# Two output products instead of three for four of eight scan tiles, with the scan's steps paced by VectorE's time

## The chip, the cores and the metric

One core of a Trainium2 chip runs the whole program. The metric is the device time of one execution in microseconds (us), as the median of several runs. Three runs of the kernel before gave 2316.76, 2317.06 and 2318.68 us, a median of 2317.06.

## The reference, cut to what matters

One decoder layer is computed for 304 tokens at once: 16 meta tokens, 256 prompt tokens, and 8 samples of 4 tokens. All of it is in fp32.

```python
x = x + 0.5 * swiglu(rmsnorm(x, norm_ffn1), ...)       # D 2048, D_FF 5632
z = rmsnorm(x, norm_mix) @ w_in                        # [u_pool | u_ssm | gate_a | gate_b]
a = pool_mix(u_pool)                                   # window means of 2, 4, 8, 16 tokens, minus u, times pool_w
s = s5_scan(u_ssm)                                     # below
s = gelu(s); s = s * sigmoid(s @ glu_w + glu_b)
m = sigmoid(gate_a) * (a @ w_branch_a) + sigmoid(gate_b) * (s @ w_branch_b)
x = x + m @ w_out
x = x + 0.5 * swiglu(rmsnorm(x, norm_ffn2), ...)
y = rmsnorm(x, final_norm)
# s5_scan: 64 groups of 16 channels, 64 complex states each
bu = einsum('blgc,gpc->blgp', u, b_bar)                # input product
h[t] = lam_bar * h[t-1] + bu[t]                        # complex, per state
y = einsum('blgp,gcp->blgc', h, c_mat).real + d * u    # output product
```

## The kernel before

**Weights.** Every weight matrix is read in blocks of 128x1024 in one fixed order (`weight_order`). SyncE's queue brings a block into one of `RAW` = 3 buffers (`raw`). ScalarE casts it to its high part (`whi`, line 161), and VectorE subtracts that from the block to get the rest (`wlo`, line 172). There are four buffers for each part. A *group* is the 24 matmuls that use one block: high part times high part, high times low, low times high (`mm3`, lines 252 to 254). Nearly all of TensorE's time goes into groups.

**Steps.** The program is recorded in an order written by hand; each engine runs its instructions in that order. After each group `step` records: the cast of the block three groups ahead (`high`), the work that waited for finished columns (`g.post`), the rest of that block (`low`), the next load, and then some *side work* from a generator. The rate `g.rate` says how many yields of the generator go into one step, one unit for one yield whatever it costs.

**The mixer.** `w_in`'s columns come first, in pairs of 128, in the order `COLS`: 0 to 3 feed the pooling branch and 4 to 7 the scan. Then come the four `pool_w` products, eight rounds of gate a with `w_branch_a` (six groups each), eight rounds of gate b (four groups each), the `glu_w` groups, and `w_branch_b`.

**The pooling.** `Pool.run` is side work on VectorE and ScalarE at 3.5 yields a step while the columns run. Its tiles are called `pt`, its results `Y`.

**The scan.** `Scan.run` is the side work after that, at `MIXRATE` = 1.53 yields a step, from the end of column 5 (the sixth of `COLS`). The states lie in 8 *row tiles* of two *halves*. A half is one tile `row` of three planes of 2x304: the input products `bu` of a tile fill planes 1 and 2 (`into`; ScalarE copies them out of PSUM). `rows` lists a half's eight steps, all on VectorE: a sum of planes 1 and 2 into plane 0 (608 elements a partition, line 965), all three planes times the rotation table `ee` (1824, line 966), a difference (1216, line 949, and a small line 951), two recurrences (`scan`, 608, line 955), a sum (576, line 971), all planes times the table again (1728, line 959: the *turned states*), and the final states out of them (36, line 962: `states`). The true parts of a state are differences of two of these planes. They are never formed for all tokens: the *output product* `outof` multiplies each of the three planes with its own 128x32 matrix and adds in PSUM (`yps`, line 914), 12 fp32 matmuls, which the profile counts as 24. It stands behind the third step of the next tile. `act` then puts gelu on it: seven small operations, to and fro between VectorE and ScalarE (`gy`, `gw`, `Y`).

Of the kernel before, what the change touches and what calls it, by code (L numbers as in the profile page):

```python
# [33 lines left out]
AHEAD = 2  # L34
RAW = 3
SETRATE = 1.25
MIXRATE = 1.53
WP = 1024
# [8 lines left out]
NCON = NT + NTV + 2  # L47
POOLRATE = 3.5
LATE = 8
STIR = 7  # L50
LAG = 0
MIXLAG = 2
COLS = (0, 1, 2, 4, 3, 5, 6, 7)
MAGIC = 12582912.0
# [128 lines left out]
def setup(ctx, tc, I):  # L183
    g = Ctx()
    nc = tc.nc
    g.tc, g.nc, g.I = tc, nc, I
    g.uid = 0
    g.side, g.rate, g.owed, g.post = None, 0, 0.0, []
# [12 lines left out]
    g.vec = g.const.tile([P, NVEC], F32, name="vec")  # L201
    return g
# [29 lines left out]

# [7 lines left out]
def also(g, more):  # L240
    g.side = more if g.side is None else chain(g.side, more)


def drain(g):
    while g.side is not None:
        if next(g.side, None) is None:
            g.side = None

# [590 lines left out]


class Scan:

# [8 lines left out]
    def input(self, ps, r):  # L851

        u = self.sp.tile([P, NT], F32, name=nm(self.g, "u"))
        self.g.nc.vector.tensor_tensor(u, ps, r, ALU.mult)
        self.u.append(u)
        if len(self.u) == 1:
            self.stored(0)
            self.stacked(0)
# [17 lines left out]
    def stored(self, i):  # L876

        g, nc = self.g, self.g.nc
        hi = self.sp.tile([P, NT], F32R, tag="uhi", name=nm(g, "uhi"), bufs=1)
        lo = self.sp.tile([P, NT], F32R, tag="ulo", name=nm(g, "ulo"), bufs=1)  # L880
        nc.scalar.copy(hi, self.u[i])
        nc.vector.tensor_tensor(lo, self.u[i], hi.bitcast(F32), ALU.subtract)
        for k, u in enumerate((hi, lo)):
            nc.gpsimd.dma_start(g.usc[i][k], u)
# [8 lines left out]
    def into(self, i, pair, ri, half, long=False):  # L893

        g = self.g
        if "row" not in pair[half]:
            pair[half]["row"] = self.sp.tile([P, 3, JB, NT], F32, tag="row", name=nm(g, "row"), bufs=4)
        row = pair[half]["row"][:, 1 + ri]
        for jj in range(JB):
            q = half * JB + jj  # L900
            ps = bank(g, "bu", aux=True, pool=g.pslong if long and jj else None)[:, :NT]
            g.nc.tensor.matmul(ps, self.bs[i][:, q, ri * P:(ri + 1) * P], self.up[:, q], start=True, stop=True)  # L902
            g.nc.scalar.copy(row[:, jj], ps)

    def outof(self, i, pair):
# [3 lines left out]
        c = self.cs[i].rearrange("p i (q c) -> p i q c", c=32)  # L909
        for k, h in enumerate((2, 1, 0)):  # L910
            for half, s in enumerate(pair):
                for jj in range(JB):
                    q = half * JB + jj
                    g.nc.tensor.matmul(self.yps[i][q * 32:q * 32 + 32], c[:, h, q], s["row"][:, h, jj, NMETA:],  # L914
                                       start=k == 0, stop=k == 2)

# [16 lines left out]
    def rows(self, sb, s):  # L933
# [23 lines left out]
        def back():  # L957
            x, e = (y.rearrange("p k j t -> p (k j) t")[:, :, NMETA:] for y in (row, ee))
            tt(x, x, e, ALU.mult)

        def states():
            tt(self.st[:, :, :, js].rearrange("p r k j -> p r j k"), both(one[:, :, S0 - 1::NS]),
               two[:, :, :, S0 - 1::NS], ALU.subtract)

        return [lambda: tt(fl(one), fl(two[:, 0]), fl(two[:, 1]), ALU.add),
                lambda: tt(row.rearrange("p k j t -> p (k j t)"), row.rearrange("p k j t -> p (k j t)"),
                           ee.rearrange("p k j t -> p (k j t)"), ALU.mult),
                turned,
                lambda: scan(2),
                lambda: scan(1),  # L970
                lambda: tt(one[:, :, NMETA:], two[:, 1, :, NMETA:], two[:, 0, :, NMETA:], ALU.add),
                back,
                states]

# [17 lines left out]
    def run(self):  # L992
# [4 lines left out]
        for i in range(KW):  # L997
            nxt = [{} for _ in range(half)]
            for h in range(half):
                sb = i * half + h  # L1000
                rows = self.rows(sb, pair[h])
                if sb >= 1 and sb + 1 < nb:
                    new = self.load(sb + 1)
                    (nxt[0] if h else pair[1])["ee"] = new["ee"]
                for n, row in enumerate(rows):
                    row()
                    if h == 0 and n == 2 and done is not None:
                        self.outof(i - 1, done)
                        acts = self.act(i - 1)
                    if h == 0 and n == 5 and i + 1 < KW:  # L1010
                        self.matrices(i + 1, ins=False)
                    k, late = divmod(h * len(rows) + n - 4, 3)
                    if i + 1 < KW and late == 0 and 0 <= k < 4:
                        self.into(i + 1, nxt, 1 - k % 2, k // 2)
                    if h == 0 and n == 1 and i + 2 < KW:
                        self.stored(i + 2)
                    if h and n == 6 and i + 2 < KW:
                        self.stacked(i + 2)
                        self.matrices(i + 2, outs=False)
                    while acts and h * len(rows) + n >= acts[0][0]:  # L1020
                        acts.pop(0)[1]()
                    yield 1
            done, pair = pair, nxt
        for _ in range(3):
            yield 1
        self.outof(KW - 1, done)
        yield 1
        for n, f in self.act(KW - 1):
            f()
            if n in (5, 7):  # L1030
                yield 1

# [5 lines left out]
class Pool:  # L1038


    def __init__(self, g, O):
# [9 lines left out]
        t2 = T()  # L1051
        self.f = [cut(t2, 0), cut(t2, 1)]
        self.LE = LE

# [3 lines left out]
    def run(self, p, pss, norm, out):  # L1058
# [6 lines left out]
        for u, end in zip(self.u, e):  # L1065
            nc.scalar.copy(end[:, :, HIST:], u[:, S0:].rearrange("p (b s) -> p b s", s=NS))
        yield 1
        for f in range(2):
# [4 lines left out]
    def means(self, w, u, e, out):  # L1073
# [4 lines left out]
        while k < w:  # L1078
# [3 lines left out]
            s, es, k, a = s2, e2, 2 * k, a ^ 1  # L1082
            yield 1
# [3 lines left out]
        yield 1  # L1087
        out.append(split(g, d, NL, "Y"))
        yield 1

# [7 lines left out]
def mixer(g, norm, O, ps0):  # L1098
# [8 lines left out]
    def gate(ps, c):  # L1107
        z = Z()[:, :NL]
        nc.vector.tensor_tensor(z, ps, norm.r[:, NMETA:], ALU.mult)
        nc.scalar.activation(z, z, AF.Sigmoid, bias=vcol(g, "b_gate", c))  # L1110
        return z

    with ExitStack() as cm:
        g.mix = cm.enter_context(g.tc.tile_pool(name="mix", bufs=1))
        with ExitStack() as cs:
# [3 lines left out]
            dparts, aparts = [], []  # L1119
            g.side, g.rate = None, POOLRATE  # L1120
            def spare(c):
                if c == KD // KC - 1:
                    g.owed -= MIXLAG

            for p in COLS:
                if p < KW // 2:
                    pool.fetch(p)
                before = {KW // 2 + 1: scan.begin, KW - 1: spare}.get(p)
                ps = proj(g, "w_in", p * 256, norm.x, NT, KD, before) if p else ps0
# [3 lines left out]
                else:  # L1133
                    g.post += [lambda q=q: scan.input(q, norm.r) for q in ps]
                if p == 1:
                    scan.first()
                if p == KW // 2 + 1:
                    drain(g)
                    g.side, g.rate = scan.run(), MIXRATE
                    g.owed = -LAG * MIXRATE  # L1140
            def mixed():
                g.owed -= MIXLAG
                for q in range(4):
# [4 lines left out]
                    for f in range(2):  # L1148
                        ps = bank(g, "pw")[:, :NL]
                        for k in range(2):  # L1150
# [3 lines left out]
                        g.post.append(lambda i=2 * q + f, ps=ps: aparts.append(  # L1154
                            split(g, ps, NL, "Y", vcol(g, "pool_scale", i))))
                    if q % 2:
                        step(g)

            mixed()
            for p in range(KD // 2):  # L1160
# [5 lines left out]
                def gated(p=p, z=z, pa=pa):  # L1166
                    for f in range(2):
                        nc.vector.tensor_tensor(z[f], pa[f], z[f], ALU.mult)
                        nc.sync.dma_start(msc[2 * p + f], z[f])

# [337 lines left out]
```

## Time and profile before

| what | value |
|---|---|
| median of three runs | 2317.06 us |
| the profiled execution's own time | 2318.77 us |
| its span | 2316.8 us |
| TensorE busy | 2306.3 us, 100% of the span |
| VectorE busy | 1576.1 us, 68% |
| ScalarE busy | 942.9 us, 41% |
| matmul records of the output products | 192, in eight bursts of 24 |

The profiled execution lies 1.71 us above the median of the three runs, and 1.97 us above its own span. The share of VectorE is an average: by the page's fortieths of the span it is busy for 40 to 80% in most of the program, and 90% or more of five of them in the middle. That is the mixer, from about 985 to 1290 us, and there the change works.

### The profile page before, as it was taken

What the parts mean: (1) busy time and instruction counts of PE and PEld (TensorE: products, weight loads), DVE (VectorE), ACT (ScalarE), POOL (GpSimd) and SP (SyncE); (2) the same over time, 40 slices, a digit from 0 to 9 for tenths busy, and PEclk for the clock granted to TensorE, in tenths of its full rate; (3) what the DMA queues carried; (4) which work ended last, traced back from release to release, by engine and by line L of the source; (5) the groups of instructions that cost most, each with busy time, mean ns of one, the idle gap of its engine ahead of it and who ended that gap; (6) DMA issues with size and microseconds to landing.
All of it is one profiled execution on the core that took longest, in us unless ns stands there. A gap on an engine that the chain in (4) does not pass through costs nothing.

```text
span 2316.8 us, 41582 instructions
## 1 busy us (share of the span) xinstructions
PE 2306.3 (100%) x17073; PEld 2293.3 (99%) x17073; DVE 1576.1 (68%) x2303; ACT 942.9 (41%) x1316; POOL 134.8 (6%) x255
## 2 busy tenths in 40 slices
PE   9999999999999999999999999999999999999998
PEld 9999999999999999999999999999999999999998
DVE  7788777877654557799999765545555555555556
ACT  5333333343333335454444544433333333333333
POOL 0000000002200002211110130000000000000001
PEclk9999999999999999999999999999999999999999
DMA  6445555556654446767785775444444444444543
GB/s 230 160 151 188 197 209 205 189 202 212 203 174 160 156 155 214 238 220 246 258 265 199 235 264 175 163 167 162 172 164 166 167 168 164 164 165 166 169 159 128
DMA packets 133454, 437.36 MB, mean 189 GB/s; under 512 B 22064, under 2 KB 33632, under 8 KB 133136
## 3 DMA queue, kind: packets, MB, share of 16 engines
q1 hardware_dynamic: 107088, 375.51, 47.6%
q0 software_dynamic: 25792, 58.87, 8.4%
q8 instruction: 134, 2.20, 0.4%
q14 instruction: 56, 0.46, 0.1%
q10 hardware_dynamic: 384, 0.32, 0.0%
HBM read 403.07 MB, written 31.55 MB: 188 GB/s over the span
## 4 chain that ended last, share of the span: by engine, by line
PE 98%; DVE 1%; issue 0%; ACT 0%; DMA 0%; SPq 0%; ACTq 0%; DVEq 0%
PE pj L253 24%; PE pj L252 24%; PE pj L254 24%; PE dn L254 8%; PE dn L252 8%; PE dn L253 8%; PE yps L914 1%; PE bu L902 0%; DMA pk<-in_first 0%; PE o L1245 0%; DVE row L955 0%; DVE wlo L172 0%; PE pw L253 0%; PE pw L252 0%; PE pw L254 0%
## 5 line engine op out<-in xcount | busy, mean ns | idle before, releaser
L172 DVE TENSOR_TENSOR wlo<-raw,whi 128x1024 fp32r<-128x1024 f32 (+1 forms) x697 | 849.6, 1220 | 576.5 <-ACT whi L161 575.6
L161 ACT CAST whi<-raw 128x1024 fp32r<-128x1024 f32 (+1 forms) x697 | 729.1, 1048 | 1202.6 <-PE pj L253 690.7
L252 PE MATMUL pj<-X,whi 128*128 128x304 f32 (+1 forms) x2428 | 728.3, 300 | 0.7 <-ACT whi L151 0.7
L253 PE MATMUL pj<-X,whi 128*128 128x304 f32 (+1 forms) x2428 | 728.2, 300 | 0.0
L254 PE MATMUL pj<-X,wlo 128*128 128x304 f32 (+1 forms) x2428 | 727.8, 300 | 0.0
L253 PE MATMUL pj<-Y,whi 128*128 128x288 f32 x1728 | 510.6, 296 | 0.0
L252 PE MATMUL pj<-Y,whi 128*128 128x288 f32 x1728 | 509.4, 295 | 0.0
L254 PE MATMUL pj<-Y,wlo 128*128 128x288 f32 x1728 | 508.8, 294 | 0.0
L252 PEld LDWEIGHTS pj<-X,whi 128*128 128x128 f32 x2428 | 457.2, 188 | 4.0 <-issue 2.1
L253 PEld LDWEIGHTS pj<-X,whi 128*128 128x128 f32 x2428 | 456.6, 188 | 0.1
L254 PEld LDWEIGHTS pj<-X,wlo 128*128 128x128 f32 x2428 | 456.3, 188 | 0.2
L252 PEld LDWEIGHTS pj<-Y,whi 128*128 128x128 f32 x1728 | 325.1, 188 | 0.9 <-issue 0.5
L253 PEld LDWEIGHTS pj<-Y,whi 128*128 128x128 f32 x1728 | 324.9, 188 | 0.0
L254 PEld LDWEIGHTS pj<-Y,wlo 128*128 128x128 f32 x1728 | 324.6, 188 | 0.0
L254 PE MATMUL dn<-H,wlo 128*128 128x304 f32 x704 | 213.0, 303 | 0.0
L252 PE MATMUL dn<-H,whi 128*128 128x304 f32 x704 | 212.8, 302 | 0.0
L253 PE MATMUL dn<-H,whi 128*128 128x304 f32 x704 | 212.2, 301 | 0.0
L254 PE MATMUL dn<-X,wlo 128*128 128x288 f32 x688 | 203.0, 295 | 0.0
L253 PE MATMUL dn<-X,whi 128*128 128x288 f32 x688 | 203.0, 295 | 0.0
L252 PE MATMUL dn<-X,whi 128*128 128x288 f32 x688 | 202.7, 295 | 0.0
L253 PEld LDWEIGHTS dn<-H,whi 128*128 128x128 f32 x704 | 132.4, 188 | 0.0
L252 PEld LDWEIGHTS dn<-H,whi 128*128 128x128 f32 x704 | 132.3, 188 | 0.0
(278 smaller groups left out, 1816.5 us busy)
## 6 DMA issues: line engine op xcount, KB each, us to landing
raw<-in_ffn_w_gate SPq DMA_DIRECT2D x175, 512.0 KB, 3.3
raw<-in_ffn_w_up SPq DMA_DIRECT2D x175, 512.0 KB, 3.3
raw<-in_ffn_w_down SPq DMA_DIRECT2D x168, 512.0 KB, 3.3
raw<-in_w_in SPq DMA_DIRECT2D x96, 512.0 KB, 4.3
raw<-in_w_out SPq DMA_DIRECT2D x32, 512.0 KB, 3.9
esc<-ee POOLq DMA_DIRECT2D x16, 912.0 KB, 5.7
ee<-esc POOLq DMA_DIRECT2D x16, 912.0 KB, 5.9
raw<-in_w_branch_a SPq DMA_DIRECT2D x16, 512.0 KB, 4.2
```

The source lines that it names most:

```text
L161: self.g.nc.scalar.copy(hi[:, :kn], self.raw[i][:, :kn])
L172: self.g.nc.vector.tensor_tensor(lo[:, :kn], raw[:, :kn], hi[:, :kn].bitcast(F32), ALU.subtract)
L252: mm(ps, wh, x[0], start=start, stop=False)
L253: mm(ps, wh, x[1], start=False, stop=False)
L254: mm(ps, wl, x[0], start=False, stop=stop)
L914: g.nc.tensor.matmul(self.yps[i][q * 32:q * 32 + 32], c[:, h, q], s["row"][:, h, jj, NMETA:], start=k == 0, stop=k == 2)
```

## The change

Five parts.

1. For row tiles 3, 4, 5 and 6 (`DIRECT`) the eighth step subtracts plane 0 from planes 1 and 2 over all 288 live tokens (1152 elements a partition, line 985). ScalarE then copies the final states with a sign (line 986) and `outof` needs two planes, 8 matmuls where it had 12.
2. Each yield returns its cost in us of VectorE, and a step's budget is the time of a group less the rest of a block: 3.186 - 1.135 us for 288 tokens, 3.355 - 1.135 for 304. VectorE's other work is taken off the budget where it is recorded, and TensorE's scan products are added to it.
3. The columns stand in the order 0, 4, 1, 5, 2, 3, 6, 7, so the scan begins after the fourth of them and no longer after the sixth. The pooling has a lane of its own (`front`) that goes first; nothing is drained at the scan's begin.
4. Four raw buffers for three.
5. The pooling's result tiles are taken at its begin.

```diff
-RAW = 3
+RAW = 4
-MIXRATE = 1.53
+LOWUS, SHORTUS, LONGUS = 1.135, 3.186, 3.355
+TIGHT = 0.0
+DIRECT = (3, 4, 5, 6,)
-COLS = (0, 1, 2, 4, 3, 5, 6, 7)
+COLS = (0, 4, 1, 5, 2, 3, 6, 7)
...
 def step(g):
...
     g.owed += g.rate
     while g.owed >= 1.0:
-        g.owed -= 1.0
-        got = next(g.side, None) if g.side is not None else None
-        if got is None:
-            g.side = None
+        cost = ahead(g)
+        if cost is None:
+            g.owed = min(g.owed, 1.0)
+            break
+        g.owed -= cost
+def ahead(g):
+    for lane in ("front", "side"):
+        gen = getattr(g, lane)
+        cost = next(gen, None) if gen is not None else None
+        if cost is not None:
+            return cost
+        setattr(g, lane, None)
...
     def outof(self, i, pair):
-        for k, h in enumerate((2, 1, 0)):
+        used = (2, 1) if i in DIRECT else (2, 1, 0)
+        g.owed += 0.54 * len(used)
+        for k, h in enumerate(used):
...
     def rows(self, sb, s):
+        def direct():
+            x = two[:, :, :, NMETA:]
+            tt(x, x, both(one[:, :, NMETA:]), ALU.subtract)
+            nc.scalar.activation(st, two[:, :, :, S0 - 1::NS], AF.Copy, scale=-1.0)
+        last = (1.33, direct) if sb * JB // 4 in DIRECT else (0.14, states)
...
+                (1.59, turned),
+                (1.335, lambda: scan(2)),
+                (1.335, lambda: scan(1)),
...
+                (1.88, back),
+                last]
...
 def mixer(g, norm, O, ps0):
-            g.side, g.rate = None, POOLRATE
+            g.side, g.rate = None, LONGUS - LOWUS
...
                 if p == KW // 2 + 1:
-                    drain(g)
-                    g.side, g.rate = scan.run(), MIXRATE
-                    g.owed = -LAG * MIXRATE
+                    g.side, g.owed = scan.run(), 0.0
+            g.rate = SHORTUS - LOWUS - TIGHT
```

How the order of instructions moves is shown at three places. On TensorE, before, the output product of row tile 3, between two groups (`row` and `cs` are its planes and matrix):

```order
L254 MATMUL pj_12719<-X_9555,wlo_12616 128x288
L914 MATMUL yps_12756<-row_11939,cs_11978 32x288 x2
L914 MATMUL yps_12756<-row_12098,cs_11978 32x288 x2
L914 MATMUL yps_12756<-row_11939,cs_11978 32x288 x2
L914 MATMUL yps_12756<-row_12098,cs_11978 32x288 x2
L914 MATMUL yps_12756<-row_11939,cs_11978 32x288 x2
L914 MATMUL yps_12756<-row_12098,cs_11978 32x288 x2
L252 MATMUL pj_12718<-X_9602,whi_12662 128x288
```

and now:

```order
L262 MATMUL pj_12514<-X_9752,wlo_12507 128x288
L931 MATMUL yps_12624<-row_11775,cs_11784 32x288 x2
L931 MATMUL yps_12624<-row_11934,cs_11784 32x288 x2
L931 MATMUL yps_12624<-row_11775,cs_11784 32x288 x2
L931 MATMUL yps_12624<-row_11934,cs_11784 32x288 x2
L260 MATMUL pj_12513<-X_9798,whi_12539 128x288
```

One plane of two halves is gone, four matmuls of twelve; so it is in tiles 4, 5 and 6.

On VectorE, before, at the end of a half of a middle tile (`z` are gate columns, `gw` a step of `act`):

```order
L172 TENSOR_TENSOR wlo_12873<-raw_12752,whi_12871 128x1024
L959 TENSOR_TENSOR row_12383<-row_12383,ee_12476 128x6x288
L927 SCALAR_TENSOR_TENSOR gw_12770<-gw_12770,gy_12769 128x288
L962 TENSOR_TENSOR states<-row_12383 128x2x2x9
L1109 TENSOR_TENSOR z_12915<-pj_12718,rs_y_10103 128x288
L1109 TENSOR_TENSOR z_12918<-pj_12719,rs_y_10103 128x288
L172 TENSOR_TENSOR wlo_12921<-raw_12801,whi_12913 128x1024
```

and now, at the end of tile 3's first half:

```order
L976 TENSOR_TENSOR row_11775<-row_11775,ee_11866 128x6x288
L944 SCALAR_TENSOR_TENSOR gw_12154<-gw_12154,gy_12153 128x288
L171 TENSOR_TENSOR wlo_12267<-raw_12136,whi_12265 128x1024
L985 TENSOR_TENSOR row_11775<-row_11775 128x4x288
L1195 TENSOR_TENSOR z_12225<-pj_12197,z_12225 128x288
L1195 TENSOR_TENSOR z_12228<-pj_12198,z_12228 128x288
L171 TENSOR_TENSOR wlo_12312<-raw_12186,whi_12306 128x1024
```

The difference of 1152 elements stands where the small one of 36 stood. Two gate products stand between it and the next rest in five of the eight halves; in the other three (tile 5's second, both of tile 6) the next rest follows at once. On ScalarE the copy of the states stands ahead of the cast for that rest.

On VectorE, now, at the scan's first half, between the columns of the pooling (`pt`, `Y`: pooling; `row`: scan):

```order
L1108 TENSOR_TENSOR pt_10012<-pt_10011 128x265
L1109 TENSOR_TENSOR pt_10015<-pt_10015 128x8x12
L1112 SCALAR_TENSOR_TENSOR pt_10010<-pt_10011,pt_10009 128x256
L1113 SCALAR_TENSOR_TENSOR pt_10010<-pt_10015,pt_10013 128x32
L1118 TENSOR_TENSOR Y_10027<-pt_10010,Y_10026 128x288
L976 TENSOR_TENSOR row_10396<-row_10396,ee_10209 128x6x288
L171 TENSOR_TENSOR wlo_10834<-raw_10718,whi_10832 128x1024
L981 TENSOR_TENSOR states<-row_10396 128x2x2x9
L989 TENSOR_TENSOR row_10403<-row_10403 128x608
L990 TENSOR_TENSOR row_10403<-row_10403,ee_10211 128x1824
```

Before, all of the pooling stood ahead of the scan's first instruction. From the scan's first instruction on VectorE to its last full step, the order now has 93 rests for 86 before, and 92 groups on TensorE for 85.

More of the change, by code (lines that the diff above doesn't have):

```diff
@@ L240, in also @@
 def also(g, more):
-    g.side = more if g.side is None else chain(g.side, more)
+    g.front = more if g.front is None else chain(g.front, more)
 def drain(g):
-    while g.side is not None:
-        if next(g.side, None) is None:
-            g.side = None
+    while ahead(g) is not None:
+        pass
 def mm3(g, ps, wh, wl, x, start, stop):
@@ L838, in ssm_setup @@
                     yield 1
+INTO = (4, 7, 10, 13)
+VIEWED = (5, 7, 9)
 class Scan:
@@ L854, in input @@
         self.g.nc.vector.tensor_tensor(u, ps, r, ALU.mult)
+        self.g.owed -= 0.38
         self.u.append(u)
@@ L882, in stored @@
         nc.vector.tensor_tensor(lo, self.u[i], hi.bitcast(F32), ALU.subtract)
+        g.owed -= 0.39
         for k, u in enumerate((hi, lo)):
@@ L903, in into @@
             g.nc.scalar.copy(row[:, jj], ps)
+            g.owed += 0.14
     def outof(self, i, pair):
@@ L914, in outof @@
                     g.nc.tensor.matmul(self.yps[i][q * 32:q * 32 + 32], c[:, h, q], s["row"][:, h, jj, NMETA:],
-                                       start=k == 0, stop=k == 2)
+                                       start=k == 0, stop=k == len(used) - 1)
     def act(self, i):
@@ L959, in back @@
             tt(x, x, e, ALU.mult)
+        st = self.st[:, :, :, js].rearrange("p r k j -> p r j k")
         def states():
[L962 to L973, printed above, removed]
+            tt(st, both(one[:, :, S0 - 1::NS]), two[:, :, :, S0 - 1::NS], ALU.subtract)
+        def direct():
[3 more added lines that the diff above has]
+        last = (1.33, direct) if sb * JB // 4 in DIRECT else (0.14, states)
+        return [(0.70, lambda: tt(fl(one), fl(two[:, 0]), fl(two[:, 1]), ALU.add)),
+                (1.97, lambda: tt(row.rearrange("p k j t -> p (k j t)"), row.rearrange("p k j t -> p (k j t)"),
+                                  ee.rearrange("p k j t -> p (k j t)"), ALU.mult)),
+                (1.59, turned),
+                (1.335, lambda: scan(2)),
+                (1.335, lambda: scan(1)),
+                (0.70, lambda: tt(one[:, :, NMETA:], two[:, 1, :, NMETA:], two[:, 0, :, NMETA:], ALU.add)),
+                (1.88, back),
+                last]
     def first(self):
@@ L1004, in run @@
                     (nxt[0] if h else pair[1])["ee"] = new["ee"]
-                for n, row in enumerate(rows):
+                for n, (cost, row) in enumerate(rows):
                     row()
-                    if h == 0 and n == 2 and done is not None:
+                    at = h * len(rows) + n
+                    if at == 2 and done is not None:
                         self.outof(i - 1, done)
                         acts = self.act(i - 1)
-                    if h == 0 and n == 5 and i + 1 < KW:
+                    if at == 5 and i + 1 < KW:
                         self.matrices(i + 1, ins=False)
-                    k, late = divmod(h * len(rows) + n - 4, 3)
-                    if i + 1 < KW and late == 0 and 0 <= k < 4:
+                    if i + 1 < KW and at in INTO:
+                        k = INTO.index(at)
                         self.into(i + 1, nxt, 1 - k % 2, k // 2)
-                    if h == 0 and n == 1 and i + 2 < KW:
+                    if at == 1 and i + 2 < KW:
                         self.stored(i + 2)
-                    if h and n == 6 and i + 2 < KW:
+                    if at == 14 and i + 2 < KW:
                         self.stacked(i + 2)
                         self.matrices(i + 2, outs=False)
-                    while acts and h * len(rows) + n >= acts[0][0]:
-                        acts.pop(0)[1]()
-                    yield 1
+                    while acts and at >= acts[0][0]:
+                        n, f = acts.pop(0)
+                        f()
+                        cost += 0.0 if n in VIEWED else 0.39
+                    yield cost
             done, pair = pair, nxt
-        for _ in range(3):
-            yield 1
+        for _ in range(2):
+            yield 2.0
         self.outof(KW - 1, done)
-        yield 1
+        yield 1.5
         for n, f in self.act(KW - 1):
             f()
-            if n in (5, 7):
-                yield 1
+            if n in VIEWED[:2]:
+                yield 1.5
     def store(self, O):
@@ L1052, in __init__ @@
         self.f = [cut(t2, 0), cut(t2, 1)]
+        self.parts = [(part(g, "Y", NL), part(g, "Y", NL)) for _ in range(KW)]
         self.LE = LE
@@ L1066, in run @@
             nc.scalar.copy(end[:, :, HIST:], u[:, S0:].rearrange("p (b s) -> p b s", s=NS))
-        yield 1
+        yield 0.77
         for f in range(2):
@@ L1086, in means @@
             ALU.mult, ALU.subtract)
-        yield 1
-        out.append(split(g, d, NL, "Y"))
-        yield 1
+        yield 0.45
+        hi, lo = self.parts[len(out)]
+        g.nc.scalar.copy(hi, d)
+        tt(lo, d, hi.bitcast(F32), ALU.subtract)
+        out.append((hi, lo))
+        yield 0.37
     def keep(self, p):
@@ L1109, in gate @@
         nc.vector.tensor_tensor(z, ps, norm.r[:, NMETA:], ALU.mult)
+        g.owed -= 0.37
         nc.scalar.activation(z, z, AF.Sigmoid, bias=vcol(g, "b_gate", c))
@@ L1127, in mixer @@
                     pool.fetch(p)
-                before = {KW // 2 + 1: scan.begin, KW - 1: spare}.get(p)
+                before = scan.begin if p == KW // 2 + 1 else None
                 ps = proj(g, "w_in", p * 256, norm.x, NT, KD, before) if p else ps0
@@ L1155, in mixed @@
                             split(g, ps, NL, "Y", vcol(g, "pool_scale", i))))
+                        g.owed -= 0.40
                     if q % 2:
```

14 lines of the change are left out of this document (4 added, 10 removed).

## The prediction

> **What bounds the kernel now.** I read the page's first lines, then TensorE's waits, then the scan's stretch.
>
> ```profile
> PE 2306.3 (100%) x17073; PEld 2293.3 (99%) x17073; DVE 1576.1 (68%) x2303; ACT 942.9 (41%) x1316; POOL 134.8 (6%) x255
> ...
> DVE  7788777877654557799999765545555555555556
> ...
> PE 98%; DVE 1%; issue 0%; ACT 0%; DMA 0%; SPq 0%; ACTq 0%; DVEq 0%
> ```
>
> TensorE is never idle; a change gains only by taking work from it. After the program's begin the list of TensorE's waits has one row inside the mixer:
>
> ```profile
> PE yps L914 <- DVE row L959: 0.5, 1, 0.5
> ```
>
> But VectorE, 68% over the span, is full in five fortieths. What counts there is its *lead*: how long before TensorE's first use a rest `wlo` is ready. From the timelines, the rests paired with their groups in order, three pairs (start us, us): at the scan's first half, at the lowest point, at the scan's last half.
>
> ```profile
> 979.74 1.22 DVE L172 TENSOR_TENSOR wlo<-raw,whi 128x1024 fp32r<-128x1024 f32 x1
> ...
> 988.14 0.30 PE L252 MATMUL pj<-X,whi 128*128 128x304 f32 x1
> ...
> 988.42 0.30 PE L254 MATMUL pj<-X,wlo 128*128 128x304 f32 x1
> ...
> 988.70 0.30 PE L253 MATMUL pj<-X,whi 128*128 128x304 f32 x1
> ...
> 1238.32 1.21 DVE L172 TENSOR_TENSOR wlo<-raw,whi 128x1024 fp32r<-128x1024 f32 x1
> ...
> 1239.10 0.29 PE L253 MATMUL pj<-X,whi 128*128 128x288 f32 x1
> ...
> 1239.63 0.36 PE L254 MATMUL pj<-X,wlo 128*128 128x288 f32 x1
> ...
> 1279.16 1.22 DVE L172 TENSOR_TENSOR wlo<-raw,whi 128x1024 fp32r<-128x1024 f32 x1
> ...
> 1282.48 0.29 PE L254 MATMUL pj<-X,wlo 128*128 128x288 f32 x1
> ```
>
> The lead is 7.46 us (988.42 less 980.96), then 0.10, then 2.10. The kernel before lives just inside VectorE's limit: the chain of waits leaves TensorE there and runs over VectorE and ScalarE to the product that waited.
>
> ```profile
> 1240.68 1.23 DVE wlo L172
> 1241.91 1.88 DVE row L959
> 1243.83 1.65 PE yps L914 x20
> ```
>
> VectorE's own stretch between the first and the last of those rests, from the table by windows and its waits there:
>
> ```profile
> 980.96:1280.38 299.42, 298.91 (x2315) 290.55 (x2313) 286.22 (x320) 144.84 (x236) 36.20 (x68) 1.00 0.74 237
> ...
> DVE wlo L172 <- ACT whi L161: 10.1, 12, 1.4
> ```
>
> Of 299.4 us VectorE (third pair) works 286.2 and stands 13.2; 10.1 of that in 12 waits for a cast. TensorE's 85 groups took 294.1 (988.42 to 1282.48). The difference, 5.4, is the lead that went.
>
> **Two output products.** This is the gain. TensorE's chain has a burst of 24 records, and what the next matmul takes after one:
>
> ```profile
> 1062.70 1.59 PE yps L914 x24
> 1064.29 0.33 PE pj L252
> ```
>
> A record takes 1.59 / 24 = 0.066 us. Four tiles lose 8 each, 32 x 0.066 = 2.1 us. The 0.33 behind a burst stays, as all eight bursts do. With the 0.5 that TensorE waited, 2.6 us can be had, and no more.
>
> **The difference on VectorE.** Durations overlap a little, so I take starts. Nearest are the sum of 576 elements, the rest and the states, and beside them the form of 1216:
>
> ```profile
> 1109.76 0.75 DVE L971 TENSOR_TENSOR row<-row 128x576 f32<-128x576 f32 x1
> 1110.43 0.82 DVE L1109 TENSOR_TENSOR z<-pj,rs_y 128x288 f32<-128x288 f32 x2
> ...
> 1114.67 1.22 DVE L172 TENSOR_TENSOR wlo<-raw,whi 128x1024 fp32r<-128x1024 f32 x1
> 1115.81 0.22 DVE L962 TENSOR_TENSOR states<-row 128x36 f32<-128x36 f32 x1
> 1115.94 0.79 DVE L965 TENSOR_TENSOR row<-row 128x608 f32<-128x608 f32 x1
> ...
> 1117.02 0.82 DVE L1168 TENSOR_TENSOR z<-pj,z 128x288 f32<-128x288 f32 x2
> 1117.75 1.22 DVE L172 TENSOR_TENSOR wlo<-raw,whi 128x1024 fp32r<-128x1024 f32 x1
> ...
> L949 DVE TENSOR_TENSOR row<-row 128x1216 f32<-128x1216 f32 x16 | 22.7, 1419 | 0.1
> ```
>
> A rest takes 1.14 from start to start, the states 0.13, a pair of `z` 0.73, and every instruction hands over some 0.08 before its end. 1152 elements lie between 576 (0.67 from start to start) and 1216 (1.42 less 0.08): 1.30, from 1.27 to 1.35. Eight of them cost 10.4, the eight states saved 1.1.
>
> A page of the Trainium skill speaks against all such counts: VectorE: DVE Perf Modes, "The DRAIN you can't avoid", says that the next instruction does not start until the pipe is empty. By it each instruction would take its full duration, 320 x 0.08 = 26 us more in this stretch, and TensorE would have waited over 20 us before the change. The trace has 0.5, and a rest of 1.22 is followed after 1.14; the measurement decides, and the sum stays.
>
> **The earlier scan.** The order now has 92 groups from the scan's first rest to its last where it had 85, since the scan starts two columns earlier. TensorE: 192 matmuls of 304 more, 24 of 288 fewer (0.140 and 0.133 from start to start: 988.14 to 988.70 and 1239.10 to 1239.63 are four each), 56 product records fewer (32 gone, 24 of the last tile behind the end), one turn behind a burst fewer, 0.2: 294.1 + 26.9 - 3.2 - 3.7 - 0.2 = 313.9 us. VectorE: seven rests more, 8.0; two `z` fewer, -0.7; the pooling of the columns 2 and 3, that stood ahead of the scan. Its 12 forms from 905 to 985 us, first and last:
>
> ```profile
> L278 DVE TENSOR_TENSOR Y<-pt,Y 128x288 fp32r<-128x288 f32 x8 | 3.7, 458 | 3.5 <-ACT Y L277 3.5
> ...
> L1081 DVE TENSOR_TENSOR pt<-pt 128x32 f32<-128x32 f32 x2 | 0.4, 186 | 0.0
> ```
>
> Those two columns' 44 instructions are 15.7 us of the 12 forms' 26.1, less 44 x 0.08: 12.2. So VectorE has 286.2 + 8.0 - 0.7 + 12.2 + 10.4 - 1.1 = 315.0 us of work beside 313.9 of TensorE's. That is what the new budget says by itself: costs equal to the starts above, 100% of the time, with nothing left for standing. Before, it was 286.2 of 294.1.
>
> **Standing.** Keep the 13.2. Then VectorE needs 328.2, and TensorE's time with a lead of 7.5 gives 321.4: TensorE waits 6.8 us for rests. Whether those waits go is seen from what ScalarE did ahead of them. Twice the cast itself waited for its raw block, elsewhere it mostly stood behind small steps of the scan:
>
> ```profile
> 1063.52 1.05 ACT L161 CAST whi<-raw 128x1024 fp32r<-128x1024 f32 x1 [5.01 <-DMA raw<-in_w_in]
> 1064.60 1.23 DVE L172 TENSOR_TENSOR wlo<-raw,whi 128x1024 fp32r<-128x1024 f32 x1 [1.00 <-ACT whi L161]
> ...
> 1078.28 0.45 ACT L928 ACTIVATE gw<-gw 128x288 f32<-128x288 f32 x1 [3.08 <-DVE gw L927]
> 1078.62 1.03 ACT L161 CAST whi<-raw 128x1024 fp32r<-128x1024 f32 x1
> 1079.69 1.23 DVE L172 TENSOR_TENSOR wlo<-raw,whi 128x1024 fp32r<-128x1024 f32 x1 [1.31 <-ACT whi L161]
> ...
> 1206.89 1.05 ACT L161 CAST whi<-raw 128x1024 fp32r<-128x1024 f32 x1 [6.79 <-DMA raw<-in_w_in]
> 1207.97 1.23 DVE L172 TENSOR_TENSOR wlo<-raw,whi 128x1024 fp32r<-128x1024 f32 x1 [0.90 <-ACT whi L161]
> ```
>
> The fourth raw buffer takes away the first and the third, 1.9 us; no less than 0, no more than 10.1. The middle one is what the new copy of the states does: ScalarE waits for the difference, copies (some 0.2), casts (0.95), hands over, and VectorE stands 1.3 us at the next rest. Eight new such places: three with nothing between cost 1.3 each, five have two gate products of 0.73 between and cost 0.55 each, 6.6 in all; from 0, if VectorE has other work there, to 10.4. I take 6.6, since the middle rows are the same chain.
>
> The rest costs nothing: the pooling's lane and its result tiles add no instruction, and since that lane goes first its results are no later for `pool_w`. Queues: POOL's loads of `ee` keep their place two halves ahead, and SP's loads only start sooner. Both cost nothing while the 16 DMA engines are free a quarter of the time (0.74 above).
>
> **Sum.** TensorE's wait is 6.8 + 6.6 - 1.9 = 11.5 us, against a gain of 2.6: +8.9. The profiled execution took 2318.77 us, that gives 2327.7; the median lies 1.7 lower, 2317.06, and gives 2326.0.
>
> **Rivals.** *The pace holds.* If VectorE stands less than 313.9 + 7.5 - 315.0 = 6.4 us in the stretch, TensorE never waits, and the time is 2317.06 - 2.6 = 2314.5. For it: in the same stretch ScalarE waits long for blocks, and the fourth buffer could give back more than the two waits I traced.
>
> ```profile
> ACT whi L161 <- DMA raw<-in_w_in: 35.7, 15, 6.8
> ```
>
> Against it: VectorE stands 13.2 now, and most of the casts that it waits for had their block. The Trainium skill's page Trainium Kernel Development and Optimization, "Best Practices", asks for double buffers so that transfers overlap work, which would favour this rival; the trace shows three buffers already in use, and no wait of TensorE for a block.
>
> *A part of it.* VectorE stands between 6.4 and 13.6 us, with what the copies add counted in, TensorE waits up to 7.2, the time lies within 0.2% of before: 2314.5 to 2321.7.
>
> *The product waits, not the rests.* Plane 1 and 2 are complete one difference later, and the product stands three steps behind it as before. The one wait of 0.5 becomes 0.5 + 1.3 in four tiles, 7.2 in all; with 2.1 saved and the old 0.5 gone, 2321.7, on the bound itself. Against it: three steps of the next half stand between, and before the change that hid the product in seven tiles of eight.
>
> **Chances.** 0.2% is 4.6 us, about what a measurement of this kernel can tell from no change. My forecast, waits for rests above 7.2 us: 0.59. The product: 0.06, half of it slower. A part: 0.16. The pace holds: 0.17. Faster by over 0.2% would need TensorE's own work to shrink by more than 2.6 us, and nothing does that: 0.02. So slower 0.62, the same 0.36. The range goes from the pace that holds (2314) to copies at their full 10.4 with the lead's lowest point 2.0 below its end, as before: 6.8 + 10.4 + 2.0 - 2.6 = +16.6, cut to 2332 since the fourth buffer gives something back. The forecast's own range is 2321.7 to 2332.
>
> **What would show it.** 160 product records for 192; a form of 1152 at about 1.35 us; TensorE waiting in sum some 12 us for rests between 1080 and 1270 us, first small, then growing; VectorE without idle but for casts, each behind a copy or a `gw`; ScalarE's waits for blocks mostly gone. I am wrong if VectorE's idle time in the scan falls below 6 us, or the difference takes clearly less than 1.3.

## The result, and the profile after

The changed kernel takes 2336.94 us (median of 4 runs, 2333.75 to 2337.92) where the kernel before took 2317.11 on the same chip (2316.76 to 2318.68, 4 runs): ratio 1.0082, 95% interval 1.0064 to 1.0099. It is slower, as forecast, but by 19.8 us and not by 8.9, and it lies 4.9 us above the top of the range.

The profiled execution took 2337.39 us, its span is 2335.6. The page's busy times, then TensorE's waits (in sum, times, longest):

```profile
PE 2312.4 (99%) x17041; PEld 2297.9 (98%) x17041; DVE 1586.2 (68%) x2303; ACT 942.9 (40%) x1324; POOL 134.9 (6%) x255
```

```profile
PE pw L260 <- DVE u L866: 5.1, 1, 5.1
PE bu L916 <- DMA usc<-uhi: 3.9, 1, 3.9
PE yps L931 <- DVE row L985: 2.8, 2, 1.9
PE pj L260 <- DVE z L1140: 1.2, 1, 1.2
...
PE pj L262 <- DVE wlo L171: 0.9, 2, 0.7
```

32 matmul records are gone (17073 to 17041), so the products were saved. But where there was one wait of 0.5 us in the mixer there are five rows. The two largest stand at the scan's begin, where I had looked for nothing; the rests `wlo`, for which I had forecast some 12 us, have 0.9.

Beside the waits TensorE was slow for a time. TensorE's windows of 3.41 us (window, its length, busy us and matmuls, granted clock, two columns on the DMAs), cut where the clock changes:

```profile
934.27:937.69 3.42, 1.51 (x11) 1.00 1.18 305
937.69:941.10 3.41, 1.44 (x6) 0.50 0.85 256
941.10:944.51 3.41, 3.41 (x15) 0.50 0.04 11
...
1009.36:1012.78 3.42, 0.10 (x1) 1.00 1.15 268
1012.78:1016.19 3.41, 1.65 (x7) 0.50 0.98 369
1016.19:1019.60 3.41, 3.41 (x16) 0.50 0.39 116
1255.16:1258.57 3.41, 1.47 (x13) 1.00 0.54 111
1258.57:1261.98 3.41, 3.41 (x19) 0.50 0.99 384
```

Behind each longer wait the clock is granted at half for 3.4 or 6.8 us. TensorE works 1.44 + 3.41 + 1.65 + 3.41 + 3.41 = 13.3 us in these windows. A matmul of 304 tokens takes 0.253 us from start to start there (941.06 to 944.10 are twelve) and 0.140 at the full clock, so 45% of that, 6.0 us, is lost. From 900 to 1500 us the sums of TensorE's busy time are, of before and of after:

```profile
sum 600.00, PE 599.49; mean PE 99.92
```

```profile
sum 600.00, PE 586.05; mean PE 97.67
```

13.4 us more of idle time, 6.0 of clock, less 2.1 of products make 17.3; the span grew by 18.8, and the rest is not accounted for.

The first wait comes out of POOL's queue. Its issues in the changed kernel at the scan's begin:

```profile
919.23 1.07 POOL L876 DMA_DIRECT2D ee<-esc  x2
...
922.38 0.54 POOL L898 DMA_DIRECT2D usc<-uhi  x1 [1.54 <-ACT uhi L894]
...
933.21 0.56 POOL L905 DMA_DIRECT2D us<-usc  x1 [9.75 <-DMA usc<-uhi]
```

```profile
939.66 1.35 PE L916 MATMUL bu<-us,bs 96*128 96x304 f32 x4 [3.88 <-DMA usc<-uhi]
```

The scan's first loads, two `ee` of 912 KB each, are now issued 3 us ahead of the small store `usc` (152 KB), from which `us` is read back for the first input product. The store is waited for until 933.21, 10.3 us after its issue was over. Before, the `ee` stood 28 us ahead of it, and the same step took 2.5 us (949.54 to 952.02). The loads have not moved (919.23 us, 920.47 before); the earlier scan brought the store forward to them:

```profile
920.47 1.11 POOL L863 DMA_DIRECT2D ee<-esc  x2
...
949.00 0.54 POOL L884 DMA_DIRECT2D usc<-uhi  x1 [8.27 <-ACT uhi L881]
...
952.02 1.64 POOL L891 DMA_DIRECT2D us<-usc  x3 [1.94 <-DMA usc<-uhi]
```

Two things can hold the store there, its place in the queue behind the loads, or the DMA engines, which were busy all the time from 922.92 to 933.21 (share 1.03) and less so from 949.54 to 952.02 before (0.84). No run separates the two.

The second wait is VectorE's order. The product `pw` needs the two PSUM banks that the last column left, and VectorE empties them (`u`) only behind the steps of the scan. VectorE after, from the last rest that stands ahead of them:

```profile
1009.57 1.22 DVE L171 TENSOR_TENSOR wlo<-raw,whi 128x1024 fp32r<-128x1024 f32 x1
...
1010.84 0.78 DVE L989 TENSOR_TENSOR row<-row 128x608 f32<-128x608 f32 x1
1011.66 2.06 DVE L990 TENSOR_TENSOR row<-row,ee 128x1824 f32<-128x1824 f32 x1
1013.63 0.47 DVE L895 TENSOR_TENSOR ulo<-u,uhi 128x304 fp32r<-128x304 f32 x1
1014.02 0.85 DVE L866 TENSOR_TENSOR u<-pj,rs_y 128x304 f32<-128x304 f32 x2
```

Before, a reserve of two steps was kept for this place (`spare`, `MIXLAG`), and `u` followed the rest at once:

```profile
1000.87 1.22 DVE L172 TENSOR_TENSOR wlo<-raw,whi 128x1024 fp32r<-128x1024 f32 x1
1002.00 0.85 DVE L854 TENSOR_TENSOR u<-pj,rs_y 128x304 f32<-128x304 f32 x2
```

The change took the reserve out, and the prediction did not speak of it.

### The profile page after: what moved, and what is told of

Read it like the earlier page. It is cut to its first block, busy times and chain, and to the rows that moved or that the text cites. A ratio compares the mean times of both kernels' runs of the same rounds, so it can differ in the third digit from the quotient of the medians.

```text
span 2335.6 us, 41518 instructions
## 1 busy us (share of the span) xinstructions
PE 2312.4 (99%) x17041; PEld 2297.9 (98%) x17041; DVE 1586.2 (68%) x2303; ACT 942.9 (40%) x1324; POOL 134.9 (6%) x255
```

## The experiments

"Repairs" below are two edits of the changed kernel's begin: the first loads earlier, and a reserve for the last column. The kernel before had medians from 2317.11 to 2317.90 in these runs.

### The begin

First theory: the two waits at the begin are a cause of their own. Second: they only uncover that VectorE is short, and what is repaired there comes back later. `e1_first_early`:

```diff
+                if p == 0:
+                    scan.first()
 ...
-                if p == KW // 2:
-                    scan.first()
```

> The scan's first loads (matrices and two tables of 912 KB) are issued on POOL's queue at the first column instead of right behind column 4; all else as in the changed kernel. Theory 1, separate causes: the input product's wait of 3.9 us and the 6.8 us at half clock behind it (3.4 us lost) go, 7.3 us in all: 2329.6 us. Theory 2, one shortage of VectorE (the balance of the prediction): the wait gave VectorE time that it now lacks, and comes back at the pooling's product or in the scan: 2334 to 2337 us. Theory 3, the column order itself leaves too little time between the input and its product: the wait stays, 2337.

2329.77 us (2329.38 to 2330.35). The wait for `usc` is gone, with the half clock at 938: 7.2 us for an edit that moves six loads in POOL's queue. That the loads' place was the cause of this wait is shown. A part of the 7.2 is the clock's: three windows at half clock are gone and not the two at 938. The wait for `u`, 5.1 us as before, has one behind it where it had two, and the one at 1258 is gone.

`e2_spare`, `g.owed -= 4.0` in the last group of the last column, alone:

> The changed kernel, with 4.0 us of budget taken off at the last group of column 7, so that no scan step stands ahead of the last two input columns on VectorE (before the change two units were taken off there). Theory 1: the wait of the first pooling product, 5.1 us, and its 6.8 us at half clock (3.4 us lost) go: 2337 - 8.5 = 2328.4 us. Theory 2: they come back in the scan, since that wait is what restored VectorE's lead from 3 to 11 us: 2334 to 2337 us.

2335.88 us. The wait for `u` falls from 5.1 to 1.8, yet nearly all of it comes back: rests 3.7, gate banks 2.5. Here the second theory held. Both together, `e3_both`:

> Both edits together. Theory 1: only the scan's own 5.0 us of waits and 1.7 us of clock are left: 2337 - 15.8 = 2321.1 us. Theory 2: the prediction's balance holds once the two early waits are gone, so TensorE waits 11.5 us in the scan: 2317.1 - 2.6 + 11.5 = 2326.0 us, more if the clock drops behind those waits.

2330.92 us, 4.9 above what the second theory gave. In TensorE's waits the begin is down to 1.8, and the scan has the shortage that was hidden behind it:

```profile
PE pj L262 <- DVE wlo L171: 3.7, 6, 1.1
PE pj L260 <- DVE z L1140: 2.5, 1, 2.5
PE pw L260 <- DVE u L866: 1.8, 1, 1.8
```

`e4_both_tight` takes 0.15 us from each step's budget (`TIGHT = 0.15`):

> Both edits, and the budget of a step 0.15 us smaller (TIGHT = 0.15), so that VectorE has about 14 us for standing over 92 steps. If the balance is right (work equal to the time, and 13 to 20 us of standing on top), nearly all waits in the scan go: 2314.5 to 2317 us. If the waits in the scan come from something other than the pace: as with both edits alone.

2337.87 us, beyond both theories: the rests are nearly in time (one wait, 1.5 us), and the last product is late (`PE yps L931 <- DVE row L976`, 13.2 us, with 17 us of half clock behind it). A slower pace only moves the shortage.

### Which part is it?

`e5_direct_alone` is the kernel before with the direct path, `e6_pace_alone` the repaired kernel with `DIRECT = ()`, `e7_raw4_alone` the kernel before with `RAW = 4`.

> The kernel before with the turned states of the row tiles 3 to 6 on VectorE and two output products there, and nothing else: the old pace by counts, the old order of columns, three raw buffers, the old reserves. Theory 1 (VectorE is too short for the difference, whatever the pace): the scan's stretch had 286.2 us of VectorE's work and 13.2 of standing beside 294.1 of TensorE's with a lead of 7.5; eight differences less eight states are 9.3 more, 2.1 of the products go: TensorE waits 286.2 + 9.3 + 13.2 - 292.0 - 7.5 = 9.2 us in many places, and with a half clock behind one or two of them the time is 2317.7 - 2.1 + 9 to 14 = 2325 to 2330, the waits being for rests and for the product. Theory 2 (what the changed kernel lost is the order of its begin and of its pace): no more than 2 us of waits, 2315 to 2318.

2335.47 us (2335.37 to 2335.60), ratio 1.0075 (1.0060 to 1.0090): 5.5 us beyond the first theory's range. TensorE's two largest waits, of which the first was one that no theory had:

```profile
PE bu L903 <- ACT row L904: 5.9, 3, 2.3
PE yps L916 <- DVE row L969: 3.7, 3, 1.8
```

The input product waits for ScalarE to empty a bank, and ScalarE's own longest waits are for the difference, ahead of the new copy of the states:

```profile
ACT states L970 <- DVE row L969: 37.5, 8, 8.0
```

> The changed kernel with the scan's first loads issued ahead, with the reserve of 4 us for the last column's banks, and with no row tile on the direct path: three output products everywhere, the states formed as before; the pace by VectorE's time, the new order of columns and four raw buffers stay. Theory 1 (VectorE is short because of the difference): 9.3 us less on VectorE and 2.1 more on TensorE, so 305.7 of work beside 316; the waits inside the scan go, the 1.8 us for the last column's banks stays: 2317 to 2320. Theory 2 (the earlier start packs too much into the stretch by itself): waits for rests of over 3 us stay, 2322 or more.

2320.80 us (2320.06 to 2322.68), ratio 1.0013 (1.0004 to 1.0022), 0.8 us above the first theory's range. Without the direct path the new pace, order and buffers together cost 3 us, mostly in waits at two places (1.8 for `u`, 1.7 for `bs`).

> The kernel before with four raw buffers for three, and nothing else. By both theories TensorE waited 0.5 us there and can gain no more: 2317.2 to 2318.2. What is looked for is ScalarE's wait for raw blocks in the scan, 35.7 us in 15 places before: under 10 us if the fourth buffer is what removed it.

2316.73 us, ratio 0.9996 (0.9986 to 1.0005), no difference that this measurement shows. ScalarE's wait for raw blocks fell from 35.7 us to 16.4, not to under 10.

### The copies on ScalarE

What the fifth kernel's rows suggest, I tried from both sides. `e9_both_states` is `e3_both` with the states formed by VectorE, ahead of the difference:

```diff
+            states()
             x = two[:, :, :, NMETA:]
             tt(x, x, both(one[:, :, NMETA:]), ALU.subtract)
-            nc.scalar.activation(st, two[:, :, :, S0 - 1::NS], AF.Copy, scale=-1.0)
```

> The changed kernel with both repairs of its begin (2330.9 us), and the states of the four direct row tiles formed by VectorE ahead of the difference, as in the other tiles, in place of the copy on ScalarE behind it; their 0.14 us are in the pace. VectorE gets 8 x 0.13 = 1.1 us more work, ScalarE loses eight copies that wait for the difference. Theory 1 (VectorE's time is what is short): nothing is won, 2330 to 2333. Theory 2 (the copies, which stand ahead of casts and of the emptying of banks on ScalarE, make a good part of the waits): 2324 to 2328.

2317.96 us (2316.51 to 2318.49, 10 runs): 13.0 us less, with some 1.1 us more work on VectorE, and 6 us below what the second theory gave. Every wait inside the scan is gone. `e10_alone_states` makes the same edit in `e5_direct_alone`:

> The kernel before with the direct path in the row tiles 3 to 6 and nothing else (2335.5 us with the copies on ScalarE), the states formed by VectorE ahead of the difference. Theory 1 (VectorE's time): the 14.5 us of waits stay, 2334 to 2338. Theory 2 (the copies on ScalarE): the 5.9 us for ScalarE's emptying of banks go and some of the rests' and the gate's, 2325 to 2330.

2326.43 us, 9.0 less; the wait for ScalarE's rows is gone. This lies in the first range of `e5_direct_alone` (2325 to 2330): without the copies the difference cost what that sum gave. `e11_copies` adds the copies alone, without the difference, to `e6_pace_alone`:

```diff
+            if sb * JB // 4 in (3, 4, 5, 6):
+                nc.scalar.activation(dum, st, AF.Copy)
```

> The kernel with the changed pace and no direct tile (2320.8 us), with eight copies of 36 elements added on ScalarE into a tile that nothing reads, each behind VectorE's last step of a half in the row tiles 3 to 6, where the changed kernel has its copies: ScalarE's wait without the difference. Theory 1 (the copies cost nothing by themselves): 2320 to 2322. Theory 2 (they delay casts and the emptying of banks): 2324 or more, with waits of TensorE for ScalarE's rows or for rests.

2329.10 us, 8.3 more. Eight copies of 36 elements, 0.27 us each, 2.2 us of ScalarE's time that lies beside other work, cost TensorE nearly four times that. How they do it stands in the changed kernel's timelines, ScalarE first, then VectorE:

```profile
1147.51 1.03 ACT L160 CAST whi<-raw 128x1024 fp32r<-128x1024 f32 x1
1152.67 0.28 ACT L986 ACTIVATE states<-row 128x36 f32<-128x36 f32 x1 [4.13 <-DVE row L985]
1152.84 0.71 ACT L917 COPY row<-bu 128x304 f32<-128x304 f32 x2
1153.44 0.45 ACT L945 ACTIVATE gw<-gw 128x288 f32<-128x288 f32 x1
1153.78 1.04 ACT L160 CAST whi<-raw 128x1024 fp32r<-128x1024 f32 x1
```

```profile
1151.28 1.35 DVE L985 TENSOR_TENSOR row<-row 128x1152 f32<-128x1152 f32 x1
1152.55 0.81 DVE L1195 TENSOR_TENSOR z<-pj,z 128x288 f32<-128x288 f32 x2
1154.86 1.23 DVE L171 TENSOR_TENSOR wlo<-raw,whi 128x1024 fp32r<-128x1024 f32 x1 [1.49 <-ACT whi L160]
```

From 1148.54 on ScalarE stands at the copy, until the difference is done at 1152.6. Then it works off what piled up behind it, the emptying of two banks and a `gw`, and only then the cast. VectorE waits 1.49 us for that cast, with both gate products already done. The Trainium skill (TensorE: Matmul & The Clock Gate, the table of specifications at its head) says that ScalarE's queue is strictly first in, first out; these rows agree, since a copy that nobody is waiting for holds up a cast that somebody is.

`e12_two_tiles` is `e3_both` with two direct tiles, copies included:

> The changed kernel with both repairs and two direct row tiles (3 and 4) for four: half of the differences (5.2 us of VectorE), half of the products saved (1.1 us). With none it took 2320.8, with four 2330.9. Theory 1 in the form of my sum (VectorE falls behind only where its lead is used up): the first tiles cost nothing or gain their 0.53 each, 2319.5 to 2322.5. The rival (each difference costs as much wherever it stands): 2325 to 2327.

2322.96 us (2322.20 to 2323.93): between the two forecasts. Two tiles cost 2.2 us over none, four cost 10.1.

### What is left

`e14_begin_stays` makes the edit of `e9_both_states` in the changed kernel and leaves its begin alone; `e13_win` is `e9_both_states` with the reserve one group earlier (`KD // KC - 2` for `KD // KC - 1`); `e15_six_tiles` is that one with six direct tiles.

> The changed kernel (2336.9 us) with the states formed by VectorE ahead of the difference and nothing else: its begin stays as it was. If begin and copies are two separate causes, only the waits of 3.9 and 5.1 us and the half clock behind them stay: 2314.5 + 9.0 + about 5 = 2328.5, from 2326 to 2330. If the waits of the begin only uncover the same shortage, the two effects overlap and it lies nearer 2322 to 2325; if taking the copies alone does nothing, 2335 or more.

2328.19 us (2327.74 to 2329.16). Each cause exists without the other, but their prices overlap. The copies cost 2336.94 - 2328.19 = 8.8 us beside the begin as it was and 13.0 beside the repaired one (`e9_both_states`). The begin costs 2336.94 - 2330.92 = 6.0 us beside the copies and 2328.19 - 2317.96 = 10.2 without them, or 13.1 against the earlier reserve below (2315.07); 8.2 of that are two waits (5.1 and 3.1).

> The changed kernel with its first loads ahead, the states on VectorE, and the reserve of 4 us one group earlier, so that the last column's banks are emptied behind the sum of 576 and no longer behind the multiplication of 1728. What was left of waits, 1.8 us and a half clock of 3.4 us behind it, should go: 2318.0 - 1.8 - 1.7 = 2314.5, which is 2.1 us of products and the 0.5 of the old wait below the kernel before, about 0.14%. Rival (what is put off there is late in the scan): waits of 1 us or more inside the scan, 2316 to 2319.

2315.07 us (2314.67 to 2316.92, 11 runs) beside 2317.80, ratio 0.9988 (0.9979 to 0.9997): 2.7 us faster than the kernel before, from 0.7 to 4.9 by the interval, and 21.9 faster than the changed kernel. In TensorE's waits the mixer has one row left (`PE yps L931 <- DVE row L976`, 0.2 us).

> The same kernel as the first of this call with six direct row tiles (1 to 6) for four: two more tiles are 5.2 us more of VectorE and 1.1 us less of products. By my sum VectorE (315.0 beside 313.9) has long been full, and each further microsecond on it is one of TensorE's waits: 2318 to 2322. If VectorE has room once ScalarE no longer holds it up (it stood 6.0 us for casts in the scan without the copies, 21 with them), 2313.0 to 2314.0.

2326.96 us, beyond both ranges. It is one wait, at the scan's end, with 13.7 us of half clock behind it:

```profile
PE yps L931 <- DVE row L976: 10.6, 1, 10.6
```

VectorE's time is short: with four tiles it just suffices. VectorE's share of the 240 us from 1020 to 1260 shows it, by the windows of all engines (TensorE's, its weight loads', VectorE's, ScalarE's and POOL's busy time); the changed kernel, `e3_both`, `e9_both_states`, then `e13_win`:

```profile
1020.00:1260.00 240.00, 235.01 (x1806) 225.58 (x1805) 225.81 (x246) 113.97 (x195) 29.82 (x56) 1.00 0.72 231
```

```profile
1020.00:1260.00 240.00, 234.69 (x1794) 225.44 (x1793) 223.13 (x240) 111.59 (x192) 29.76 (x56) 0.99 0.73 232
```

```profile
1020.00:1260.00 240.00, 240.00 (x1869) 233.34 (x1868) 235.92 (x261) 116.15 (x190) 29.90 (x57) 1.00 0.76 244
```

```profile
1020.00:1260.00 240.00, 240.00 (x1858) 234.42 (x1858) 237.12 (x262) 116.65 (x190) 29.51 (x56) 1.00 0.76 244
```

VectorE stands 14.2 us in the changed kernel and 2.9 in `e13_win`. Where only the copies differ, it stands 16.9 us with them (`e3_both`) and 4.1 without (`e9_both_states`), 12.8 more, nearly the 13.0 us that they cost; beside the old begin 14.2 and 5.9 (`e14_begin_stays`), 8.3 more for a price of 8.8. In `e13_win` VectorE is 98.8% busy and TensorE does not wait for it in this stretch; six tiles ask for more, and what does not fit comes out behind the scan's end.

### The half clock

`e8_stalls`:

> The kernel before with nine stalls of TensorE added in the last feed-forward, between a gate product and the up product after it, about 57 to 76 us apart: one matmul into a free bank, a chain of 2, 4, 6, 8, 10, 13, 16, 21 and 29 copies of 128x128 on ScalarE, one matmul that reads the last copy. They change no result. By the copies of the traces (0.2 to 0.45 us for 128x288 and more) the stalls grow from about 1 us to 6 us or more. Theory 1 (the half clock follows a wait above some length, between the 1.9 us that had none and the 2.5 us that had it): no stretch of half clock behind the stalls below 2 us, one of 3.4 or 6.8 us behind each stall above 3 us. Theory 2 (it follows the amount of waiting in a longer stretch, or the place in the scan): no clear bound by length, or none here at all.

One run, 2370.01 us. The stalls were 0.68, 1.34, 2.00, 2.66, 3.32, 4.31, 5.29, 6.94 and 9.58 us. Half clock followed the third (3.4 us), not the fourth, and all from the fifth on (3.4, 3.4, 6.8, 6.8 and 10.2 us). So neither theory holds as it stands: the bound is not one of length. All stretches of half clock begin whole multiples of 3.413 us apart. TensorE's windows on that grid, at the stalls of 2.00, 2.66 and 3.32 us:

```profile
1759.69:1763.10 3.41, 1.49 (x11) 1.00 0.39 141
1763.10:1766.51 3.41, 3.41 (x16) 0.50 0.47 154
1838.21:1841.62 3.41, 1.89 (x15) 1.00 0.49 162
1841.62:1845.03 3.41, 2.27 (x17) 1.00 0.02 7
...
1920.09:1923.52 3.43, 0.40 (x3) 1.00 0.34 133
1923.52:1926.93 3.41, 3.41 (x16) 0.50 0.13 29
```

The wait of 2.66 was shared by two windows of the grid, and each was busy for 1.89 us or more; the wait of 2.00 fell into one window, which was busy for 1.49. Taken with the changed kernel's windows above: a window with at most 1.65 us of work (the 1.65 in one at half clock) is followed by one at half clock, one with 1.89 or more is not.

The waits of the other runs, on their own grids, narrow this and limit it. At the full clock, windows with 1.60, 1.61 and 1.62 us of work were followed by half clock (`e4_both_tight`, `e11_copies`, `e9_both_states`), one with 1.64 was not (`e6_pace_alone`), and one with 1.57 was not either (`e1_first_early`, 1001.24 to 1004.65). So the bound lies near 1.6 us, known to about 0.1. A window that itself runs at half clock needs more: 2.94 us of work, from 938.62 to 942.03 in `e14_begin_stays`, kept the clock at half.

With 0.253 us for a matmul instead of 0.140, 2.94 us at half clock hold the work of 1.6 at the full clock, so one bound by work fits both. That is an estimate from these rows.

## Why the prediction came out as it did

**Right.** *Two output products*: 32 records fewer, and the 2.6 us that "can be had, and no more" are had by `e13_win`, 2.7 us (0.7 to 4.9). *The difference on VectorE*: 1350 ns for one of 1152 elements, eight of them. *The sum of work*, 315.0 beside 313.9 us: in the changed kernel VectorE works 318.0 us from the scan's first step to its last (955.40 to 1295.40), and in `e13_win` it is full to 98.8%, with no room for two more tiles. (The section of the Trainium skill's page VectorE: DVE Perf Modes that the prediction set against these counts, "The DRAIN you can't avoid", adds that an instruction that is not held starts earlier, so it did not speak against them as flatly as I wrote.)

*Slower*, too, came as forecast, but in the changed kernel more by luck than by the forecast's waits. Of its 13.9 us of waits 9.0 stand at the begin, where I had none, and 0.9 are for rests. The forecast waits for rests show once the begin is repaired (3.7 in `e3_both`).

**The step that failed: "The rest costs nothing", and in it "Queues".** I wrote that POOL's loads of `ee` keep their place two halves ahead. They keep it in the scan, but the first two, with `bs` and `cs`, came to stand right ahead of the small store on which the first product hangs; and I priced SP's and POOL's queues by the free share of the DMA engines (0.74 busy). That was an average from 980.96 us on: while the store waited, they had nothing free (1.03), and an average says nothing of what stands first in one queue. The reserve for the last column's banks is in the diff, and no sentence of mine was about it. Together this was 9.0 us of waits where I had put nothing, and 6.0 to 13.1 us of time, by what else is repaired.

**What was not in the sum: the clock.** My sum turned a wait into time one for one. 13.4 us of idle time brought another 6.0 us by the half clock.

**Mis-sized, with the mechanism right: the copies.** I had ScalarE wait at the copy and VectorE stand at the next rest, 1.3 us at three places and 0.55 at five, 6.6 in all, because two gate products would cover the five. That cover was there at two of them, where VectorE stood 0.54 and 0.56. At the other three it stood 1.50, 1.49 and 1.50, because the copy was not alone ahead of the cast: the emptying of two banks and a `gw` stood between the two, as in the timeline above, and my sum did not have them. At the three places without cover VectorE stood 1.27, 2.23 and 1.47. The eight make 10.6 and not 6.6. The copies' price was 8.8 us in the changed kernel (1.5 of it clock) and 13.0 once the begin no longer let VectorE run ahead.

**Mis-sized the other way: "Keep the 13.2".** I took VectorE's standing of before as given, less 1.9 for the fourth buffer, so 11.3 us. In `e13_win` it stands 2.9 us in 240, where the kernel before stands 9.7 (busy 230.26 in the same 240). Fourth buffer, order and pace are changed together there; the fourth buffer alone gave 1.2 us in `e7_raw4_alone`, within the interval of no difference. What they do together, with the repaired begin, is seen with the direct path: without them 2326.43 (`e10_alone_states`), with them 2315.07. No run takes the pace alone. The two errors nearly cancel, which is luck: I forecast waits of 11.5 us in the scan; `e3_both`, with the begin repaired, lies 16.4 us above 2314.5, of which 1.8 is the wait for `u` and 1.5 half clock, so some 13. TensorE's rows of waits in the scan add to 7.5 of these; where the others lie is not shown.

**The rivals.** *The pace holds* (2314.5) is what the change would have done without the copies and with its begin in order (2315.07). The reason I gave for it, the fourth buffer, did nothing clear by itself; whether the new pace needs it, no run shows. *The product waits*: 2.8 us of the 13.4. The long wait with six tiles is another one: there the last tile's product, which has no difference, waits for a VectorE that is late.

**The signs I named.** 160 product records and the form of 1152 came as written; waits that grow to the end did not, since, as I read it, TensorE's waits at the begin gave VectorE a new lead twice (with both nearly gone, in `e3_both`, the rests wait 3.7 us and not 0.9). ScalarE's waits for raw blocks did not go: 17.9 us of 35.7.

## What to carry to other kernels

A small instruction on an engine off the critical path costs what stands behind it: before moving work to ScalarE because it is 40% busy, look at what it waits for there and at the next cast in that queue. When an order is changed, look at every small transfer with somebody waiting for its end, and at the large ones that now stand right ahead of it. And price a wait of TensorE with the clock that follows it, 3.4 us at half speed for each window that the wait more than half empties.

## What the runs showed of the hardware

The clock is judged in fixed windows of 3.413 us, and about half a window of work, 1.6 us in these rows, decides: a wait of 2.00 us was followed by a window at half clock, which costs some 1.5 us more at 45%, one of 2.66 by none. The Trainium skill (TensorE: Matmul & The Clock Gate, "What's actually happening") has a free-running window of 3413 ns and two clocks, half and full; the windows here agree. It puts the half clock behind a whole idle window, and its advice ("Why this matters for your kernels") is to avoid gaps over about 3 us; here 1.9 us without work inside one window were enough (3.42 less 1.51, at 934 us).

A store of 152 KB behind two loads of 912 KB in POOL's queue was waited for until 10.3 us after its issue; with the loads far ahead, 2.5 us. Whether the queue's order or the full DMA engines (1.03 busy for 0.84) held it is open.
